# Samples' x transposed once and dt kept in three chunks, and x asked for block by block behind the first split

## The chip, the cores and the metric

The kernel runs on one core of a Trainium2 chip. The metric is the device time in microseconds (us), the median of three runs. The engines are called TensorE (PE in the profile; PEld is its weight load), VectorE (DVE), ScalarE (ACT), GpSimd (POOL) and SyncE (SP, which only issues transfers here). Each takes its instructions in order.

## The reference

One inference step of one layer with two kinds of heads, on 256 prompt tokens and 8 samples of 8 new tokens (64 rows), 320 tokens in all, width 2048, all float32:

```
h    = rms_norm(x)
proj = h @ w_in                      # columns: [gMLP u | gMLP v | SSD z | SSD x,B,C | SSD dt]
gate = gelu(u) * (tril(w_s) @ layer_norm(gelu(v)) + b_s)          # inside chunks of 128 tokens
x,B,C = silu(causal_conv4(xBC));  dt = softplus(dt_raw + dt_bias);  a = -exp(a_log)
# SSD, per head (32 heads of 64, 4 groups of 8 heads, state 128):
#   state_t = exp(dt_t a) state_{t-1} + dt_t x_t B_t^T,   y_t = state_t C_t
y    = rms_norm_by_group((y + d x) * silu(z))
x    = x + rms_norm([gate | y] @ w_out)
x    = x + rms_norm(conv_ffn(rms_norm(x)))                        # conv of 3, gelu(g)*u, d_ff 5632
```

The prompt starts from a zero state. Each sample carries its own state and runs 8 tokens; the new states (8 samples x 32 heads x 64 x 128) are outputs too.

## The kernel before

**Layout and products.** Most tiles hold features on the 128 partitions and the 320 tokens along the row (256 of the prompt, then 64 of the samples). For accuracy each big product is three: a weight block is split into `whi` (rounded) and `wlo` (the rest), the activations into `h_hi` and `h_lo`, and `accumulate` (L153 to L155) issues whi x hi, whi x lo and wlo x hi. Weights come in slabs of 512 KB through `slab` (L118 transfer on SP's queue, L124 cast on ScalarE, L125 subtraction on VectorE), with three buffers. TensorE works through the stages: v columns of `w_in` by tokens (`by_tokens`, L144), B, C, x, gate u, `w_out`, z, then the FFN. Beside the products runs a list of generators, `bg`; `tick` advances the first by one step after a part of a slab, so that small work lies between products. A scheduler then sets the order on each engine by priorities; `tc.issue_after` keeps one instruction behind another on its engine.

**The start.** `xf` is the input x, 16 blocks (`kt`) of 128 features. `load_x(k, n)` (L570) asks for n blocks from block k on ScalarE's queue. Before anything else, blocks 0, 1, 2-3 and 4-5 are asked for, four transfers; the next ones go out two blocks at a time as `x_ready` splits block `kt` into `h_hi` (ScalarE, L584) and `h_lo` (VectorE, L585), and copies the samples' columns of both into `xs_two` (L591). Ten products of ones (`early`, L70) run ahead of the first real product.

**dt.** `steps` makes dt, its decays and sums. Its products `dt_ps` (L479) bring dt to tokens in five chunks of 128: prompt, prompt, samples twice over, and, for each half of the samples (four samples of 8, 32 tokens), these 32 tokens repeated four times over the 128 partitions (`dtf`, L473). All later steps on `dt`, `dec` and `sp_e` run on 5 x 32 columns. Near its end, `dec_ps` (L539 to L546) makes the sums up to the end of a chunk, for the samples with the masks `later_s` (L544, GpSimd), one of 64x128 for each half. Just ahead of these GpSimd has the copies into `cb_cms` (L773, L774), which take over the buffer of `dacsT` and so wait for the transfer out of it.

**The SSD of a group.** `ssd(g)` (four groups) brings x to tokens. `x_of_samples(i)`, called twice per group, takes half i of the samples: ScalarE writes them fourfold into `x4` (`fourfold`, L397), TensorE transposes four blocks into `xt_ps` (L393), VectorE multiplies by dt into `xq` (L824), ScalarE rounds `xq` into `xsp[:, i]` (L841), VectorE subtracts for the lower 64 partitions (L842), so that the four quarters hold x rounded, rounded, rest, rest; two more products with dt go into `xdt`. `grown` multiplies `xsp` with the matching B parts (`bm`) into `up_ps` (L904), which is added to the samples' states `st` (L906); `with_c` forms `yo_ps` (L887). The second half's `x_of_samples(1)` stands in the first turn of the loop over the states, two steps after `x_of_samples(0)`.

Of the kernel before, what the change touches and what calls it, by code (L numbers as in the profile page):

```python
# [9 lines left out]
F32 = mybir.dt.float32  # L10
# [3 lines left out]
ALU = mybir.AluOpType  # L14
# [20 lines left out]
def hybrid_step(  # L35
# [21 lines left out]
    def misc(name):  # L57
        return ms.tile([P, 512], F32, tag="ms", name=name)
# [332 lines left out]
    def by_token(ps, x, c):  # L391

        pe.transpose(ps, x[:, P * c:P * c + P], ident)  # L393
# [6 lines left out]
    with ExitStack() as mctx:  # L400
# [40 lines left out]

        dt = op.tile([P, 5, NH], F32, name="dt")
        sums = op.tile([P, 3, NH], F32, name="sums")
        dec = op.tile([P, 5, NH], F32, name="dec")
        ed = op.tile([P, 4, 4], F32, name="ed")
        tote = op.tile([P, NH, NB], F32, name="tote")

# [17 lines left out]
        def steps():  # L467

            dtf = op.tile([P, NT + NS + 2 * P], F32, tag="dtf", name="dtf", bufs=1)
            dve.tensor_tensor(out=dtf[:, :NT], in0=ps_dt[0][:, :NT], in1=r1, op=ALU.mult)  # L470
            pool.tensor_copy(dtf[:, NT:NT + NS], dtf[:, NP:NT])
            for i in range(2):
                pool.tensor_copy(dtf[:, (3 + i) * P:(4 + i) * P].rearrange("p (q t) -> p q t", q=4),  # L473
                                 dtf[:, NP + 32 * i:NP + 32 * i + 32].unsqueeze(1).to_broadcast([P, 4, 32]))
            yield
            ps = misc("dt_ps")
            for c in range(5):

                pe.matmul(ps[:, NH * c:NH * c + NH], dtf[:, P * c:P * c + P], sums[:, 0], start=True, stop=True)  # L479
            H5 = 5 * NH  # L480
            dve.tensor_tensor(out=dt, in0=ps[:, :H5].rearrange("p (c h) -> p c h", c=5),
                              in1=bias_bc.unsqueeze(1).to_broadcast([P, 5, NH]), op=ALU.add)

            e = op.tile([P, 5, NH], F32, name="sp_e")
            q = dec
            z2 = tp.tile([P, NT], F32, tag="pv", name="sp_z2", bufs=4)[:, :5 * NH].rearrange("p (c h) -> p c h", c=5)
            act.activation(e, dt, AF.Abs)
            act.activation(e, e, AF.Exp, scale=-1.0)
            dve.tensor_scalar(out=q, in0=e, scalar1=2.0, scalar2=None, op0=ALU.add)
            dve.reciprocal(q, q)  # L490
            dve.tensor_tensor(out=e, in0=e, in1=q, op=ALU.mult)
            dve.tensor_tensor(out=z2, in0=e, in1=e, op=ALU.mult)
            dve.tensor_scalar(out=q, in0=z2, scalar1=2.0 / 17, scalar2=2.0 / 15, op0=ALU.mult, op1=ALU.add)
            for n in (13, 11, 9, 7, 5, 3, 1):
                dve.tensor_tensor(out=q, in0=q, in1=z2, op=ALU.mult)
                dve.tensor_scalar(out=q, in0=q, scalar1=2.0 / n, scalar2=None, op0=ALU.add)
            yield
            dve.tensor_tensor(out=q, in0=q, in1=e, op=ALU.mult)
            dve.scalar_tensor_tensor(out=dt, in0=dt, scalar=0.0, in1=q, op0=ALU.max, op1=ALU.add)
            da = e  # L500
            ea = a_bc
            act.activation(ea, a_bc, AF.Exp)
            dve.scalar_tensor_tensor(out=da, in0=dt, scalar=-1.0, in1=ea.unsqueeze(1).to_broadcast([P, 5, NH]),
                                     op0=ALU.mult, op1=ALU.mult)
# [12 lines left out]
            p4 = ps[:, 2 * NH:3 * NH].rearrange("p (g r i) -> p g r i", g=4, r=2)  # L517
            for r in range(2):
                x_at, s_at = slice(64 - 64 * r, P - 64 * r), slice(64 * r, 64 * r + 64)
                dve.tensor_copy(n4[x_at, :, r], p4[x_at, :, r])  # L520
                act.activation(ed[s_at], p4[s_at, :, r], AF.Exp)
            yield

            ps = misc("csT_ps")
            for c in range(2):
                pe.matmul(ps[:NH, P * c:P * c + P], da[:, c], upper, start=True, stop=True)
            pe.matmul(ps[:NH, NP:NT], da[:NS, 2], upper_s[:NS], start=True, stop=True)
            dacsT = op.tile([P, NT + NS + 2 * P], F32, tag="dtf", name="dacsT", bufs=1)[:, :NT + NS]
            dve.tensor_copy(dacsT[:NH, NS:], ps[:NH, :NT])
            dve.tensor_copy(dacsT[:NH, :NS], ps[:NH, NP:NT])  # L530
            sp.dma_start(dacs_d, dacsT[:NH])
            totc = op.tile([NH, NB], F32, name="totc")
            dve.tensor_copy(totc, dacsT[:NH, :NS].rearrange("p (b t) -> p b t", b=NB)[:, :, TS - 1])
            sp.dma_start(tot_d, totc)
            yield

            ps = misc("dec_ps")
            for c in range(2):
                pe.matmul(ps[:, NH * c:NH * c + NH], later, da[:, c], start=True, stop=True)  # L539
            pe.matmul(ps[:, 2 * NH:3 * NH], ones, da[:, 1], start=True, stop=True)  # L540
            later_s = tp.tile([P, NT], F32, tag="pv", name="later_s", bufs=4)[:NS, :2 * P].rearrange("p (r q t) -> p r q t", r=2, q=4)
            for r in range(2):
                rs = slice(32 * r, 32 * r + 32)
                pool.tensor_tensor(out=later_s[:, r], in0=later[:NS, rs].unsqueeze(1).to_broadcast([NS, 4, 32]),  # L544
                                   in1=bd[:, rs].unsqueeze(1).to_broadcast([NS, 4, 32]), op=ALU.mult)
                pe.matmul(ps[:, (3 + r) * NH:(4 + r) * NH], later_s[:, r].rearrange("p q t -> p (q t)"), da[:NS, 2],  # L546
                          start=True, stop=True)
            act.activation(dec.rearrange("p c h -> p (c h)"), ps[:, :H5], AF.Exp)
            dve.tensor_tensor(out=dt[:, 3:5], in0=dt[:, 3:5], in1=dec[:, 3:5], op=ALU.mult)

            sp.dma_start(tote, tot_d.unsqueeze(0).broadcast_to([P, NH, NB]))
            act.activation(tote, tote, AF.Exp)


        with tc.tile_pool(name="gp", bufs=1) as gp:
# [13 lines left out]
                cs = slice(KD + NT * k if k else 0, KD + NT * (k + n))  # L569
                act.dma_start(flat[:, cs], xT[:, cs])  # L570
            with tc.high_priority(offset=300000):
                for k, n in ((0, 1), (1, 1), (2, 2), (4, 2)):
                    load_x(k, n)
                    if k == 1:
                        act.activation(held, ones[:, 0:1], AF.Square)

            x_split = []

            def x_ready(k0, nk):

                with tc.high_priority(offset=100000), tc.issue_after(rounded[0]) if rounded else nullcontext():
                    for kt in range(k0, k0 + nk):
# [1 line left out]
                        x_split.append(act.activation(hT[0][:, kt, :], x, AF.Copy, scale=pre[:, kt:kt + 1]).ins)  # L584
                        dve.scalar_tensor_tensor(out=hT[1][:, kt, :], in0=x, scalar=pre[:, kt:kt + 1],  # L585
                                                 in1=hT[0][:, kt, :].bitcast(F32), op0=ALU.mult, op1=ALU.subtract)
                        if kt % 2 == 0 and kt < 10:
                            with tc.issue_after(x_split[-1]):
                                load_x(kt + 6, 2)
                        for i in range(2):  # L590
                            dve.tensor_copy(xs_two[kt // 8][:, kt % 8, NS * i:NS * i + NS], hT[i][:, kt, NP:])  # L591

# [174 lines left out]
        with tc.tile_pool(name="sd", bufs=1) as sd:  # L767
# [31 lines left out]
            def ssd(g):  # L799
# [31 lines left out]
                                       in1=dec[:, i, h0:h0 + 8].unsqueeze(2).to_broadcast([P, 8, 64]), op=ALU.mult)  # L831
                    return xde

                def x_of_samples(i):
                    ps = misc("xt_ps")
                    x4 = fourfold(sd.tile([P, 4, P], F32, tag="xde", name="x4", bufs=2), xs, i)
                    for j in range(4):
                        by_token(ps[:, P * j:P * j + P], x4[:, j], 0)
                    xq = sd.tile([P, 512], F32, tag="xde", name="xq", bufs=2)
                    times(xq, ps, 3 + i)  # L840
                    act.copy(xsp[:, i], xq)  # L841
                    dve.tensor_tensor(out=xsp[64:, i], in0=xq[64:], in1=xsp[64:, i].bitcast(F32), op=ALU.subtract)  # L842
                    for r in range(2):
                        at = slice(64 - 64 * r + 32 * i, 96 - 64 * r + 32 * i)
                        times(xdt[at, 2, 256 * r:256 * r + 256], ps[at, 256 * r:256 * r + 256], 2, at, slice(4 * r, 4 * r + 4))

                for c in range(2):
                    ps = misc("xt_ps")
# [19 lines left out]
                for hb in range(2):  # L868
                    dve.tensor_tensor(out=cms[:, 4 * hb:4 * hb + 4], in0=cmask[:, 4 * hb:4 * hb + 4],
                                      in1=cT[:, g, NP + 32 * hb:NP + 32 * hb + 32].unsqueeze(1).to_broadcast([P, 4, 32]),  # L870
                                      op=ALU.mult)
                x_of_samples(0)
                yield

                ps = misc("s1_ps")
# [56 lines left out]
                for i in range(4):  # L932
# [4 lines left out]
                    if i:  # L937
                        end(i - 1)
                    yield
                    if i == 0:  # L940
                        x_of_samples(1)
                    yield
                begin(3)
                yo_to_xdt()
# [470 lines left out]
```

## Time and profile before

| What | Value |
|---|---|
| median of three runs | 1779.02 us (1778.82 to 1779.88) |
| the profiled execution's own time | 1781.37 us |
| its span | 1779.7 us |
| TensorE, VectorE, ScalarE, GpSimd busy | 99%, 66%, 46%, 15% |
| mean DMA rate over the span | 163 GB/s |

The profile is of one execution, whose own time is its span and 1.7 us around it. A line of the timeline gives start and duration in us, engine, source line, operation, and tile written from tiles read with their shapes; in square brackets stand the idle time of the engine just before and what ended it. A merged line carries "x" and a count. One float32 product with plain float32 operands shows as two records, a transpose as one. In groups, the numbers after the bar are busy us and mean ns of one.

### The profile page before, as it was taken

The page shows a single profiled execution, that of the slowest core. Times are in us where ns is not written, and L with a number is a line of the kernel's source. Part 1 is how long each engine was busy: PE and PEld are TensorE (multiplying, and loading weights), DVE is VectorE, ACT ScalarE, POOL GpSimd, SP SyncE. Part 2 cuts the span into 40 slices and gives each one's busy share as a digit, 9 for nine tenths or more (in the row PEclk, how much of TensorE's full clock was granted, in tenths as well). Part 3 has the DMA queues.
Part 4 walks back from the last instruction along what each step waited for, and adds up shares of the span by engine and source line. Part 5 has one row for each costly group of instructions (what it writes and reads, how often), then busy time and mean ns, then how long its engine had stood idle before and what let it go on. Part 6 is the DMA issues. An engine that isn't in the chain of part 4 may idle for free.

```text
span 1779.7 us, 30655 instructions
## 1 busy us (share of the span) xinstructions
PE 1770.5 (99%) x11933; PEld 1715.7 (96%) x11933; DVE 1168.0 (66%) x1999; ACT 819.5 (46%) x1195; POOL 273.5 (15%) x602
## 2 busy tenths in 40 slices
PE   9999999999999999999999999999999999999998
PEld 7789999999999998999999999999999999999998
DVE  7549764656977768677865464756656575656575
ACT  5434555334564547445545333343434343433445
POOL 1202200000331313103121011110102020101004
PEclk9999999999999999999999999999999999999999
DMA  7546645456665665554554545545545545454543
GB/s 260 163 148 177 189 128 154 153 153 188 216 190 190 181 207 168 168 171 145 180 156 146 157 149 151 155 148 152 157 144 156 150 150 155 150 150 155 147 154 107
DMA packets 214417, 289.91 MB, mean 163 GB/s; under 512 B 16384, under 2 KB 143744, under 8 KB 214080
## 3 DMA queue, kind: packets, MB, share of 16 engines
q1 hardware_dynamic: 202544, 268.74, 49.6%
q10 hardware_dynamic: 10016, 14.16, 2.2%
q0 software_dynamic: 1712, 5.05, 1.0%
q8 instruction: 94, 1.54, 0.4%
q14 instruction: 51, 0.42, 0.1%
HBM read 273.08 MB, written 14.82 MB: 162 GB/s over the span
## 4 chain that ended last, share of the span: by engine, by line
PE 97%; DVE 1%; ACT 0%; DMA 0%; issue 0%; POOL 0%; POOLq 0%; ACTq 0%; DVEq 0%
PE ps L153 19%; PE ps L155 19%; PE ps L154 19%; PE pd L153 10%; PE pd L155 10%; PE pd L154 10%; PE ps_v L144 7%; PE y_ps L983 1%; PE up_ps L904 0%; PE yo_ps L887 0%; PE sg L731 0%; PE xt_ps L393 0%; DMA cs<-dacs_d 0%; PE x1p L1278 0%; PE tsum L296 0%
## 5 line engine op out<-in xcount | busy, mean ns | idle before, releaser
L125 DVE TENSOR_TENSOR wlo<-wraw,whi 128x1024 fp32r<-128x1024 f32 (+1 forms) x476 | 582.5, 1224 | 432.4 <-ACT whi L124 430.1
L124 ACT CAST whi<-wraw 128x1024 fp32r<-128x1024 f32 (+1 forms) x475 | 494.8, 1042 | 729.9 <-PE ps L154 392.1
L153 PE MATMUL ps<-h_hi,whi 128*128 128x320 f32 x2268 | 704.0, 311 | 0.0
L154 PE MATMUL ps<-h_lo,whi 128*128 128x320 f32 x2268 | 702.7, 310 | 0.0
L155 PE MATMUL ps<-h_hi,wlo 128*128 128x320 f32 x2268 | 702.2, 310 | 0.0
L153 PEld LDWEIGHTS ps<-h_hi,whi 128*128 128x128 f32 x2268 | 426.2, 188 | 2.6 <-issue 1.6
L154 PEld LDWEIGHTS ps<-h_lo,whi 128*128 128x128 f32 x2268 | 426.3, 188 | 0.7
L155 PEld LDWEIGHTS ps<-h_hi,wlo 128*128 128x128 f32 x2268 | 426.2, 188 | 0.0
L155 PE MATMUL pd<-fhi,wlo 128*128 128x320 f32 x704 | 218.2, 310 | 0.0
L153 PE MATMUL pd<-fhi,whi 128*128 128x320 f32 x704 | 218.2, 310 | 0.0
L154 PE MATMUL pd<-flo,whi 128*128 128x320 f32 x704 | 218.2, 310 | 0.0
L153 PE MATMUL pd<-ohi,whi 128*128 128x320 f32 x448 | 139.4, 311 | 0.0
L155 PE MATMUL pd<-ohi,wlo 128*128 128x320 f32 x448 | 138.7, 310 | 0.0
L154 PE MATMUL pd<-olo,whi 128*128 128x320 f32 x448 | 138.7, 310 | 0.0
L153 PEld LDWEIGHTS pd<-fhi,whi 128*128 128x128 f32 x704 | 132.1, 188 | 0.0
L154 PEld LDWEIGHTS pd<-flo,whi 128*128 128x128 f32 x704 | 132.1, 188 | 0.0
L155 PEld LDWEIGHTS pd<-fhi,wlo 128*128 128x128 f32 x704 | 132.1, 188 | 0.0
L1180 POOL COPY ptf<-pad 128x2 f32<-128x2 f32 x88 | 21.0, 239 | 603.7 <-DVE pad L1168 603.0
L249 DVE TENSOR_TENSOR acc_ffn<-acc_ffn,pd 128x320 f32<-128x320 f32 (+1 forms) x161 | 77.5, 482 | 37.8 <-PE pd L155 36.5
L153 PEld LDWEIGHTS pd<-ohi,whi 128*128 128x128 f32 x448 | 84.1, 188 | 1.4 <-issue 1.0
L154 PEld LDWEIGHTS pd<-olo,whi 128*128 128x128 f32 x448 | 84.1, 188 | 0.3
L155 PEld LDWEIGHTS pd<-ohi,wlo 128*128 128x128 f32 x448 | 84.1, 188 | 0.1
(328 smaller groups left out, 1867.9 us busy)
## 6 DMA issues: line engine op xcount, KB each, us to landing
wraw<-in_ffn_w_up SPq DMA_DIRECT2D x176, 512.0 KB, 3.7
wraw<-in_w_in SPq DMA_DIRECT2D x140, 512.0 KB, 3.8
wraw<-in_ffn_w_down SPq DMA_DIRECT2D x88, 512.0 KB, 3.4
wraw<-in_w_out SPq DMA_DIRECT2D x64, 512.0 KB, 3.4
st<-in_state_ssm SPq DMA_DIRECT2D x32, 256.0 KB, 3.9
out_ssm_state_sample<-st ACTq DMA_DIRECT2D x30, 256.0 KB, 3.4
cs<-dacs_d SPq DMA_DIRECT2D x16, 320.0 KB, 4.7
xr<-in_xT SPq DMA_DIRECT2D x4, 640.0 KB, 4.0
```

Source lines behind the costliest of these rows:

```text
L124: rounded[:] = [act.copy(hi, raw).ins]
L125: dve.tensor_tensor(out=lo, in0=raw, in1=hi.bitcast(F32), op=ALU.subtract)
L144: made = pe.matmul(out, xi, w[g][wi], start=first and begins, stop=last and ends)
L153: pe.matmul(ps, whi, xhi, start=first, stop=False)
L154: pe.matmul(ps, whi, xlo, start=False, stop=False)
L155: return pe.matmul(ps, wlo, xhi, start=False, stop=last).ins
L249: added_last[:] = [dve.tensor_tensor(out=acc[:, nb, ts], in0=acc[:, nb, ts], in1=ps[:, ts], op=ALU.add).ins]
L983: pe.matmul(ps[64 * i:64 * i + 64, cols], w(hl), x(hl, m, cpx), tile_position=(0, 64 * i), **flags)
L1180: pool.tensor_copy(ptf[:, k, :], pad[:, 256:258])
```

## The change

Three things change. First, `dt` keeps three chunks in `steps` (two of the prompt, one of the samples), so that its steps run on 3 x 32 columns; a fourth column of `dt` and `dec`, on 64 partitions, holds the samples' decayed dt, and there is one mask `later_s` of 64x64, made ahead of the `csT_ps` products. Second, `x_of_samples` is called once per group: it transposes the 64 sample rows directly from `xs` (outputs of 64 rows), multiplies by dt once, and then fills the four quarters of both halves of `xsp` by 32-row copies: two rounded ones, a subtraction, and a copy of the rest for each half, six copies on ScalarE and two subtractions on VectorE per group. Third, only x's block 0 is asked for ahead of its split. Blocks 1 and 2-3 are asked for behind the split of block 0, blocks 4-5 and 6-7 behind that of block 1, the others as before.

In the order in which the instructions of the two built programs stand, TensorE's differs at these places only: two `dt_ps` products fewer, one `later_s` product in the insertion of the others in place of two a product apart each, one set of four sample transposes per group for two, and `up_ps` of the first samples a little earlier in groups 1 and 3. VectorE splits `h_lo` of block 0 ahead of the first `wlo`. The number of transfers of x stays at nine.

```diff
-        dt = op.tile([P, 5, NH], F32, name="dt")
+        dt = op.tile([P, 4, NH], F32, name="dt")
...
-            for i in range(2):
-                pool.tensor_copy(dtf[:, (3 + i) * P:(4 + i) * P].rearrange("p (q t) -> p q t", q=4),
-                                 dtf[:, NP + 32 * i:NP + 32 * i + 32].unsqueeze(1).to_broadcast([P, 4, 32]))
             yield
             ps = misc("dt_ps")
-            for c in range(5):
+            for c in range(3):
                 pe.matmul(ps[:, NH * c:NH * c + NH], dtf[:, P * c:P * c + P], sums[:, 0], start=True, stop=True)
...
+            later_s = tp.tile([P, NT], F32, tag="pv", name="later_s", bufs=4)[:NS, :NS]
+            pool.tensor_tensor(out=later_s, in0=later[:NS, :NS], in1=bd, op=ALU.mult)
             ps = misc("csT_ps")
...
-            for r in range(2):
-                rs = slice(32 * r, 32 * r + 32)
-                pool.tensor_tensor(out=later_s[:, r], in0=later[:NS, rs].unsqueeze(1).to_broadcast([NS, 4, 32]),
-                                   in1=bd[:, rs].unsqueeze(1).to_broadcast([NS, 4, 32]), op=ALU.mult)
-                pe.matmul(ps[:, (3 + r) * NH:(4 + r) * NH], later_s[:, r].rearrange("p q t -> p (q t)"), da[:NS, 2],
-                          start=True, stop=True)
-            act.activation(dec.rearrange("p c h -> p (c h)"), ps[:, :H5], AF.Exp)
-            dve.tensor_tensor(out=dt[:, 3:5], in0=dt[:, 3:5], in1=dec[:, 3:5], op=ALU.mult)
+            pe.matmul(ps[:NS, 3 * NH:4 * NH], later_s, da[:NS, 2], start=True, stop=True)
+            act.activation(dec[:, :3].rearrange("p c h -> p (c h)"), ps[:, :3 * NH], AF.Exp)
+            act.activation(dec[:NS, 3], ps[:NS, 3 * NH:4 * NH], AF.Exp)
+            dve.tensor_tensor(out=dt[:NS, 3], in0=dt[:NS, 2], in1=dec[:NS, 3], op=ALU.mult)
...
-                for k, n in ((0, 1), (1, 1), (2, 2), (4, 2)):
-                    load_x(k, n)
-                    if k == 1:
-                        act.activation(held, ones[:, 0:1], AF.Square)
+                load_x(0, 1)
+                act.activation(held, ones[:, 0:1], AF.Square)
...
-                        if kt % 2 == 0 and kt < 10:
-                            with tc.issue_after(x_split[-1]):
-                                load_x(kt + 6, 2)
+                        with tc.issue_after(x_split[-1]):
+                            for k, n in ((1, 1), (2, 2)) if kt == 0 else ((4, 2), (6, 2)) if kt == 1 else ((kt + 6, 2),) if kt in (2, 4, 6, 8) else ():
+                                load_x(k, n)
...
-                def x_of_samples(i):
+                def x_of_samples():
                     ps = misc("xt_ps")
-                    x4 = fourfold(sd.tile([P, 4, P], F32, tag="xde", name="x4", bufs=2), xs, i)
                     for j in range(4):
-                        by_token(ps[:, P * j:P * j + P], x4[:, j], 0)
+                        pe.transpose(ps[:NS, P * j:P * j + P], xs[:, j, NP:NT], ident)
                     xq = sd.tile([P, 512], F32, tag="xde", name="xq", bufs=2)
-                    times(xq, ps, 3 + i)
-                    act.copy(xsp[:, i], xq)
-                    dve.tensor_tensor(out=xsp[64:, i], in0=xq[64:], in1=xsp[64:, i].bitcast(F32), op=ALU.subtract)
+                    at = slice(0, NS)
+                    times(xq[at], ps[at], 3, at)
                     for r in range(2):
-                        at = slice(64 - 64 * r + 32 * i, 96 - 64 * r + 32 * i)
-                        times(xdt[at, 2, 256 * r:256 * r + 256], ps[at, 256 * r:256 * r + 256], 2, at, slice(4 * r, 4 * r + 4))
+                        times(xdt[64 - 64 * r:P - 64 * r, 2, 256 * r:256 * r + 256], ps[at, 256 * r:256 * r + 256], 2, at,
+                              slice(4 * r, 4 * r + 4))
+                    for i in range(2):
+                        here = slice(32 * i, 32 * i + 32)
+                        for q in range(2):
+                            act.copy(xsp[32 * q:32 * q + 32, i], xq[here])
+                        dve.tensor_tensor(out=xsp[64:96, i], in0=xq[here], in1=xsp[here, i].bitcast(F32), op=ALU.subtract)
+                        act.copy(xsp[96:P, i], xsp[64:96, i])
...
-                    if i == 0:
-                        x_of_samples(1)
```

More of the change, by code (lines that the diff above doesn't have):

```diff
@@ L440, in heads_in @@
             return xs
-        dt = op.tile([P, 5, NH], F32, name="dt")
+        dt = op.tile([P, 4, NH], F32, name="dt")
         sums = op.tile([P, 3, NH], F32, name="sums")
-        dec = op.tile([P, 5, NH], F32, name="dec")
+        dec = op.tile([P, 4, NH], F32, name="dec")
         ed = op.tile([P, 4, 4], F32, name="ed")
@@ L471, in steps @@
             pool.tensor_copy(dtf[:, NT:NT + NS], dtf[:, NP:NT])
-            for i in range(2):
-                pool.tensor_copy(dtf[:, (3 + i) * P:(4 + i) * P].rearrange("p (q t) -> p q t", q=4),
-                                 dtf[:, NP + 32 * i:NP + 32 * i + 32].unsqueeze(1).to_broadcast([P, 4, 32]))
             yield
             ps = misc("dt_ps")
-            for c in range(5):
+            for c in range(3):
                 pe.matmul(ps[:, NH * c:NH * c + NH], dtf[:, P * c:P * c + P], sums[:, 0], start=True, stop=True)
[L480 to L487, printed above, removed]
+            dt3 = dt[:, :3]
+            dve.tensor_tensor(out=dt3, in0=ps[:, :3 * NH].rearrange("p (c h) -> p c h", c=3),
+                              in1=bias_bc.unsqueeze(1).to_broadcast([P, 3, NH]), op=ALU.add)
+            e = op.tile([P, 3, NH], F32, name="sp_e")
+            q = dec[:, :3]
+            z2 = tp.tile([P, NT], F32, tag="pv", name="sp_z2", bufs=4)[:, :3 * NH].rearrange("p (c h) -> p c h", c=3)
+            act.activation(e, dt3, AF.Abs)
             act.activation(e, e, AF.Exp, scale=-1.0)
@@ L498, in steps @@
             dve.tensor_tensor(out=q, in0=q, in1=e, op=ALU.mult)
-            dve.scalar_tensor_tensor(out=dt, in0=dt, scalar=0.0, in1=q, op0=ALU.max, op1=ALU.add)
+            dve.scalar_tensor_tensor(out=dt3, in0=dt3, scalar=0.0, in1=q, op0=ALU.max, op1=ALU.add)
             da = e
@@ L502, in steps @@
             act.activation(ea, a_bc, AF.Exp)
-            dve.scalar_tensor_tensor(out=da, in0=dt, scalar=-1.0, in1=ea.unsqueeze(1).to_broadcast([P, 5, NH]),
+            dve.scalar_tensor_tensor(out=da, in0=dt3, scalar=-1.0, in1=ea.unsqueeze(1).to_broadcast([P, 3, NH]),
                                      op0=ALU.mult, op1=ALU.mult)
@@ L540, in steps @@
             pe.matmul(ps[:, 2 * NH:3 * NH], ones, da[:, 1], start=True, stop=True)
-            later_s = tp.tile([P, NT], F32, tag="pv", name="later_s", bufs=4)[:NS, :2 * P].rearrange("p (r q t) -> p r q t", r=2, q=4)
-            for r in range(2):
-                rs = slice(32 * r, 32 * r + 32)
-                pool.tensor_tensor(out=later_s[:, r], in0=later[:NS, rs].unsqueeze(1).to_broadcast([NS, 4, 32]),
-                                   in1=bd[:, rs].unsqueeze(1).to_broadcast([NS, 4, 32]), op=ALU.mult)
-                pe.matmul(ps[:, (3 + r) * NH:(4 + r) * NH], later_s[:, r].rearrange("p q t -> p (q t)"), da[:NS, 2],
-                          start=True, stop=True)
-            act.activation(dec.rearrange("p c h -> p (c h)"), ps[:, :H5], AF.Exp)
-            dve.tensor_tensor(out=dt[:, 3:5], in0=dt[:, 3:5], in1=dec[:, 3:5], op=ALU.mult)
+            pe.matmul(ps[:NS, 3 * NH:4 * NH], later_s, da[:NS, 2], start=True, stop=True)
+            act.activation(dec[:, :3].rearrange("p c h -> p (c h)"), ps[:, :3 * NH], AF.Exp)
+            act.activation(dec[:NS, 3], ps[:NS, 3 * NH:4 * NH], AF.Exp)
+            dve.tensor_tensor(out=dt[:NS, 3], in0=dt[:NS, 2], in1=dec[:NS, 3], op=ALU.mult)
             sp.dma_start(tote, tot_d.unsqueeze(0).broadcast_to([P, NH, NB]))
@@ L871, in ssd @@
                                       op=ALU.mult)
-                x_of_samples(0)
+                x_of_samples()
                 yield
```

## The prediction

> **What bounds the kernel now.** I read the page first, then who waits for whom, then the busy times by stretch, and last the timeline of the places that the change touches.
>
> ```profile
> span 1779.7 us, 30655 instructions
> ...
> PE 1770.5 (99%) x11933; PEld 1715.7 (96%) x11933; DVE 1168.0 (66%) x1999; ACT 819.5 (46%) x1195; POOL 273.5 (15%) x602
> ...
> PE 97%; DVE 1%; ACT 0%; DMA 0%; issue 0%; POOL 0%; POOLq 0%; ACTq 0%; DVEq 0%
> ```
>
> TensorE is busy for 99% of the span and 97% of the chain that ended last is its own. So an instruction that TensorE no longer issues is time saved in full, work on other engines counts only where TensorE waits for it, and every new wait of TensorE counts in full. In the view of TensorE's waits, no line names a weight tile; two of them name what is edited here:
>
> ```profile
> PE dec_ps L546 <- POOL later_s L544: 1.0, 2, 0.7
> PE up_ps L904 <- DVE xsp L842: 0.8, 2, 0.6
> ```
>
> The first is 1.0 us in two waits, the second 0.8 us in two. The busy times by stretch (us, then busy time and count for PE, PEld, DVE, ACT, POOL, then granted clock, DMA share, GB/s) show what stands behind the first:
>
> ```profile
> 246.80:250.20 3.40, 3.40 (x14) 3.40 (x14) 0.22 (x1) 0.38 (x2) 0.00 (x0) 0.50 0.55 154
> 250.20:254.00 3.80, 3.80 (x28) 3.80 (x27) 1.17 (x1) 1.36 (x2) 0.00 (x0) 1.00 0.00 0
> ```
>
> For 3.4 us right after the `later_s` waits the granted clock is 0.50, and half as many products fit.
>
> **Part 1: `later_s`.** GpSimd makes two 64x128 masks behind two copies into `cb_cms` that wait for the transfer of `dacsT`. TensorE alone, then GpSimd alone:
>
> ```profile
> 243.55 0.31 PE L155 MATMUL ps<-h_hi,wlo 128*128 128x320 f32 x1
> 243.70 0.53 PE L539 MATMUL dec_ps<-sp_e,later 128*128 128x32 f32 x4
> 244.06 0.39 PE L540 MATMUL dec_ps<-sp_e,ones 128*128 128x32 f32 x2
> 244.29 0.39 PE L153 MATMUL ps<-h_hi,whi 128*128 128x320 f32 x1
> 245.02 0.41 PE L546 MATMUL dec_ps<-sp_e,later_s 64*128 64x32 f32 x2 [0.34 <-POOL later_s L544]
> 245.36 0.41 PE L154 MATMUL ps<-h_lo,whi 128*128 128x320 f32 x1
> 246.46 0.41 PE L546 MATMUL dec_ps<-sp_e,later_s 64*128 64x32 f32 x2 [0.69 <-POOL later_s L544]
> 246.80 0.63 PE L155 MATMUL ps<-h_hi,wlo 128*128 128x320 f32 x1
> ...
> 250.33 0.31 PE L153 MATMUL ps<-h_hi,whi 128*128 128x320 f32 x1
> ...
> 250.92 0.31 PE L154 MATMUL ps<-h_lo,whi 128*128 128x320 f32 x1
> ```
>
> ```profile
> 243.81 0.33 POOL L773 COPY cb_cms<-ident 64x64 f32<-64x64 f32 x1 [25.68 <-PE ps L154]
> ...
> 244.52 1.89 POOL L544 TENSOR_TENSOR later_s<-later,bd 64x128 f32<-64x128 f32 x2
> ```
>
> At full clock a product follows the last by 0.147 us (250.33 to 250.92, four steps). From 243.55 to 246.80, 3.25 us, three of them start (0.44 us), so `dec_ps` costs 2.81 us. Its first insertion, of three small products, costs 0.74 - 0.15 = 0.59 us. After the change a fourth joins it, and no other insertion follows: the smaller mask is made before the `csT_ps` products, and in the order in which the changed program's instructions stand it is ahead of both copies on a GpSimd that had been idle for 25.68 us. A fourth costs 0.21 us (a fifth of the `dt_ps` row below). Saved: 2.81 - 0.80 = **2.0 us** (1.6 if the new product has an insertion of its own, 0.58 us like the one at 245.02 without its wait).
>
> From 246.80 to 250.33 thirteen products take 3.53 us in place of 1.91: the half clock costs **1.6 us** more. A stall of 0.34 and one of 0.69 us amid small products let the clock fall; the two waits for `xsp`, 0.8 us together among full products, did not. With the stalls gone I take it as gone. The Trainium skill (TensorE: Matmul & The Clock Gate, Part 1) says that the clock is halved after an idle window of about 3.4 us, and that the window runs freely. The length agrees; idle it was not, since TensorE stood still for 1.03 us of it in all. By that rule the dip hangs on where the window lies, and is a case of its own below.
>
> **Part 2: fewer products.** From the chain that ended last, in order of time:
>
> ```profile
> 212.81 1.03 PE dt_ps L479 x10
> ...
> 448.26 0.44 PE xt_ps L393 x4
> ```
>
> `dt_ps` issues three products for five: two fifths of 1.03, **0.4 us**. Each of the four head groups transposes its samples in one set of four rather than two sets. A set takes 0.44 us; four sets are **1.8 us**. The remaining sets write 64 rows and not 128. I price them as before, 0.44 us: the columns that stream through are the same 128. Were they half as dear, 0.9 us more would go.
>
> The steps on 96 columns in place of 160, and two GpSimd copies less, I price at nothing: none of these engines is waited for there. ScalarE gets six 32-row copies per group for two whole copies and two fourfold ones; at 0.6 us each that adds some 5 us, on an engine that idles for 54% of the span. If the weight casts behind these were late, TensorE would wait for weights, which it does nowhere now.
>
> **Part 3: when TensorE gets `xsp`.** It waits in groups 1 and 3, for the second half of the samples. Now both halves come from one set of transposes, and TensorE asks for both early: in group 1 right behind `yo_ps`, 24 products after the transposes. Rows of group 1 (vector, scalar, tensor), then the subtraction over all groups (least, median and most ns), and from the page the mean ns of a weight subtraction and cast:
>
> ```profile
> 513.16 0.68 DVE L824 TENSOR_TENSOR xq<-xt_ps,dt 128x512 f32<-128x512 f32 x1
> ```
> ```profile
> 513.87 0.62 ACT L841 CAST xsp<-xq 128x512 fp32r<-128x512 f32 x1 [0.82 <-DVE xq L824]
> ```
> ```profile
> 517.54 0.60 PE L393 MATMUL xt_ps<-ident,x 128*128 128x128 f32 x4
> 518.07 0.64 PE L887 MATMUL yo_ps<-st,cb_cms 128*32 128x256 f32 x8
> ```
> ```profile
> L842 DVE TENSOR_TENSOR xsp<-xq,xsp x8: 690/1004/1445, 445.8 to 704.5; 64x512 fp32r<-64x512 f32 x8
> ```
> ```profile
> L125 DVE TENSOR_TENSOR wlo<-wraw,whi 128x1024 fp32r<-128x1024 f32 (+1 forms) x476 | 582.5, 1224 | 432.4 <-ACT whi L124 430.1
> L124 ACT CAST whi<-wraw 128x1024 fp32r<-128x1024 f32 (+1 forms) x475 | 494.8, 1042 | 729.9 <-PE ps L154 392.1
> ```
>
> The second set at 517.54 is gone and `yo_ps` (0.64) takes its place, so TensorE asks at about 518.2 and 518.4. A copy's time goes by its row of 512, not by its rows: I keep 0.62 us on ScalarE and at least 0.69 on VectorE for 32 rows. ScalarE starts at 513.87; four copies and that of `s` end at 517.0. VectorE, done with `xq` at 513.84, has a weight subtraction (1.22) and two `xdt` products of half the width (0.4 each) first; it subtracts from 515.9 and ends at 517.3. The last copy ends at 517.9, in time by 0.5 us. With both subtractions at 1.445 us it would end at 519.4, and TensorE would wait 1.0 us. The Trainium skill (GPSIMD Engine Reference, Key points) says that GpSimd shares its SBUF interfaces with VectorE, in contention when VectorE has two SBUF inputs, as these subtractions have; GpSimd is busy on `st` here. The spread of the row, 690 to 1445 ns, agrees. In group 3 a weight cast (1.04) stands ahead of the last copy; by the same steps that copy ends within 0.2 us of TensorE's asking. So the old 0.8 us of waits goes, and I put 0.1 us of new ones against it, nearer to the quiet case because GpSimd's work covers only part of the two subtractions: **0.7 us** saved, between 0.8 saved and, with 1.0 us in group 1 and 0.4 in group 3, 0.6 lost.
>
> **Part 4: the start.** ScalarE's queue, then TensorE, then the landing of the second block (KB, us from issue) and those of all x transfers of the first 24 us:
>
> ```profile
> 4.23 0.33 ACTq L570 DMA_DIRECT2D vt<-in_xT  x1
> 4.61 0.56 ACT L584 ACTIVATE h_hi<-vt 128x320 fp32r<-128x320 f32 x1 [1.37 <-DMA vt<-in_xT]
> ```
> ```profile
> 9.32 0.40 PE L144 MATMUL ps_v<-whi,h_hi 128*128 128x512 f32 x1
> 9.56 0.39 PE L144 MATMUL ps_v<-whi,h_lo 128*128 128x512 f32 x1
> ```
> ```profile
> vt<-in_xT ACTq DMA_DIRECT2D x1, 160.0 KB, 4.7
> ```
> ```profile
> DMA to landing us min/median/max: 3.4/5.1/5.7
> ```
>
> The first block lands at 4.2 (the least, 3.4, after an issue at 0.8) and its split waits until 4.61 because ScalarE first issues a transfer (4.23). That issue leaves, so the split starts at 4.25. TensorE gains 0.1 us at most, since `xs_two` now stands behind `wlo` on VectorE. The second block is asked for behind that, at 4.26, and no longer right behind the first. TensorE needs its low part at 9.5 (9.56 less the gain); it comes 1.25 us after the landing (split 0.56, low part 0.55, hand-overs), so it must land by 8.2. At 3.4 us it lands at 7.7, at its own 4.7 at 9.0, at 5.7 at 10.0. No other x transfer is ahead of it, but six weight transfers are: I take 4.1, nearer to 3.4 than to 5.7, landing at 8.4: 0.2 lost, 0.1 gained, **-0.1 us**; ends +0.1 and -1.8. All later blocks are needed 3.8 us (sixteen products at 0.24) apart and come with slack. The moved issues pass nothing on SP; on ScalarE they stand ahead of two weight casts, needed only at 11.
>
> **Sum.** 2.0 + 1.6 + 0.4 + 1.8 + 0.7 - 0.1 = 6.4 us off the profiled execution's 1781.37 (span 1779.7 and 1.7 around it). That execution is 2.35 us above the median of 1779.02; I take the same 6.4 us off the median: **1772.6**.
>
> **Rivals.** *The half clock is not in the timed executions* (or stays in others): 1779.02 - 4.8 = 1774.2. For it: the profiled one is 2.35 us slower, and 1.6 of that could be this. Against: the sparse stretch is 3.2 us long, so most placings of a 3.4 us window catch much of it. 0.25.
>
> *x comes late.* At 5.7 us the start loses 1.7 us, and a stall of that size could bring 1.6 us of half clock: 1772.6 + 3.3 = 1775.9. For it: most x landings are near 5. Against: those are 320 KB each. 0.12.
>
> *The stalls stay* (`later_s` or `xsp` late in another way), and only the products go: 1779.0 - 2.2 = 1776.8. 0.07.
>
> *Slower: the chain to `xsp` runs serially.* From the samples' transposes to the last quarter: `xq` 0.69, five copies ahead of the last two 3.1, two subtractions at 1.445, two copies 1.24, and a weight cast and subtraction between, 2.27: 10.2 us. By the places of its instructions TensorE has 66, 24, 36 and 24 products (0.147 each) and two `yo_ps` (0.64 each) in between: 11.0, 4.8, 6.6 and 4.8 us. Stalls: 0 + 5.4 + 3.6 + 5.4 = 14.4 us, against 6.7 us won elsewhere (the old waits included): 1786.7. It decides from 6.7 us of stalls on. Against it: the copies need only `xq`, so they overlap the subtractions. 0.05.
>
> **Numbers.** The forecast has 0.51; its own range is 1771.3 to 1773.7. From 1771.0 to 1776.0 the range takes in the first two rivals and leaves out most of the third, the fourth, and a tail below. A measurement of this kernel can tell about 0.2%, 3.6 us: below 1775.5 is faster. Forecast, first rival and a small part of the second: 0.79 faster; the rest of the second and the third: 0.16; slower 0.05.
>
> **What would show it.** `dec_ps` in one insertion near 244 with no wait, no 0.50 clock at 247; three `dt_ps` products; sixteen sample transposes of 64 rows; `up_ps` waits under 0.4 us in all; the second x block landing near 8.4 and TensorE without a gap at 9.3. Wrong would be a wait of `up_ps` in every group, an idle TensorE with half clock in the first 20 us, or a new wait for `whi`.

## The result, and the profile after

| Kernel | median, us | executions |
|---|---|---|
| before, timed on the same chip | 1779.66 | 22 |
| changed | 1782.61 | 22 |
| changed, the profiled execution | 1783.25 (span 1781.5) | 1 |

The ratio is 1.0014 (95%: 1.0009 to 1.0020): 3.0 us slower, a small loss but one clear of its interval, where 1772.6 had been forecast. The page of the changed kernel, and its view of TensorE's waits (us in all, times, longest):

```profile
span 1781.5 us, 30593 instructions
...
PE 1770.3 (99%) x11911; PEld 1715.3 (96%) x11911; DVE 1164.1 (65%) x1987; ACT 825.2 (46%) x1204; POOL 273.5 (15%) x599
...
PE 96%; DVE 2%; ACT 1%; DMA 1%; issue 0%; ACTq 0%; DVEq 0%
```
```profile
PE up_ps L901 <- ACT xsp L842: 3.2, 3, 2.0
...
PE y_ps L978 <- PE y_ps L978: 0.5, 1, 0.5
PE yo_ps L884 <- DMA st<-in_state_ssm: 0.2, 1, 0.2
```

The 22 records less of TensorE are there (11911 for 11933), and the `later_s` waits are gone. In their place `up_ps` waits 3.2 us in three waits for the last copy into `xsp`, where it had waited 0.8. The longest is in group 2, which Part 3 of the prediction did not walk through. VectorE, ScalarE, GpSimd and TensorE there, from the timeline:

```profile
602.94 0.68 DVE L841 TENSOR_TENSOR xsp<-xq,xsp 32x512 fp32r<-32x512 f32 x1
603.66 2.15 DVE L967 TENSOR_TENSOR cs<-cs,cb_cms 128x320 f32<-128x320 f32 x3
605.73 2.08 DVE L125 TENSOR_TENSOR wlo<-wraw,whi 128x1024 fp32r<-128x1024 f32 x1
607.73 1.34 DVE L967 TENSOR_TENSOR cs<-cs,cb_cms 128x320 f32<-128x320 f32 x1
609.10 1.48 DVE L841 TENSOR_TENSOR xsp<-xq,xsp 32x512 fp32r<-32x512 f32 x1
```
```profile
610.62 0.62 ACT L842 CAST xsp<-xsp 32x512 fp32r<-32x512 f32 x1 [3.68 <-DVE xsp L841]
```
```profile
604.11 1.35 POOL L822 TENSOR_TENSOR xde<-xdt,dec 128x512 f32<-128x512 f32 x1 [2.95 <-PE s_ps L873]
605.42 3.31 POOL L895 TENSOR_TENSOR st<-st,tote 128x512 f32<-128x512 f32 x2
608.98 2.52 POOL L895 TENSOR_TENSOR st<-st,tote 128x512 f32<-128x512 f32 x2 [0.25 <-PE yo_ps L884]
```
```profile
608.81 0.51 PE L901 MATMUL up_ps<-xsp,bm 128*128 128x512 f32 x1
611.28 0.79 PE L901 MATMUL up_ps<-xsp,bm 128*128 128x512 f32 x1 [1.97 <-ACT xsp L842]
```

The second half's subtraction stands on VectorE behind four products with `cb` and a weight subtraction. Beside GpSimd's `st` the weight subtraction takes 2.08 us (mean 1.22) and the subtraction for `xsp` 1.48 in place of 0.68. ScalarE idles 3.68 us, copies, and TensorE has stood still for 1.97 us. Then, by stretch (us, busy and count for PE, PEld, DVE, ACT, POOL, granted clock, DMA share, GB/s):

```profile
604.13:607.54 3.41, 3.41 (x28) 3.02 (x21) 3.41 (x4) 2.72 (x5) 3.41 (x3) 1.00 0.00 0
607.55:610.96 3.41, 1.77 (x15) 0.84 (x13) 3.35 (x4) 0.34 (x1) 3.16 (x3) 1.00 0.53 152
610.97:614.38 3.41, 3.10 (x11) 3.01 (x12) 2.15 (x3) 1.72 (x3) 0.53 (x1) 0.50 0.40 150
614.39:617.80 3.41, 3.41 (x27) 2.71 (x26) 0.00 (x0) 1.05 (x1) 0.44 (x1) 1.00 0.76 228
```

One stretch in which TensorE was busy for 1.77 of 3.41 us, and the next runs at half the clock. A second half-clock stretch lies in the small products at the end:

```profile
1768.09:1771.49 3.40, 3.40 (x13) 3.01 (x13) 2.72 (x7) 0.43 (x1) 1.53 (x2) 0.50 0.13 48
```

Group 1 went the way of the prediction's upper bound: both subtractions at 1.5 us, all of it beside `st`, and waits of 0.30 and 0.96 us, 1.26 in all (bound: 1.0).

```profile
512.95 3.03 DVE L841 TENSOR_TENSOR xsp<-xq,xsp 32x512 fp32r<-32x512 f32 x2
```
```profile
512.91 5.01 POOL L895 TENSOR_TENSOR st<-st,tote 128x512 f32<-128x512 f32 x4
```
```profile
515.22 0.50 PE L901 MATMUL up_ps<-xsp,bm 128*128 128x512 f32 x1 [0.30 <-ACT xsp L842]
516.68 0.50 PE L901 MATMUL up_ps<-xsp,bm 128*128 128x512 f32 x1 [0.96 <-ACT xsp L842]
```

### The profile page after: what moved, and what is told of

Its sections match the earlier page's. It is cut to its first block, busy times and chain, and to the rows that moved or that the text cites. A ratio compares the mean times of both kernels' runs of the same rounds, so it can differ in the third digit from the quotient of the medians.

```text
span 1781.5 us, 30593 instructions
## 1 busy us (share of the span) xinstructions
PE 1770.3 (99%) x11911; PEld 1715.3 (96%) x11911; DVE 1164.1 (65%) x1987; ACT 825.2 (46%) x1204; POOL 273.5 (15%) x599
## 4 chain that ended last, share of the span: by engine, by line
PE 96%; DVE 2%; ACT 1%; DMA 1%; issue 0%; ACTq 0%; DVEq 0%
PE ps L153 18%; PE ps L154 18%; PE ps L155 18%; PE pd L153 10%; PE pd L154 10%; PE pd L155 10%; PE ps_v L144 6%; PE y_ps L978 1%; DMA vt<-in_xT 0%; PE up_ps L901 0%; DVE cs L967 0%; PE sg L723 0%; PE yo_ps L884 0%; DVE wlo L125 0%; DVE xsp L841 0%
```

## The experiments

Theory A: the chain that fills `xsp` ends too late, and its waits, with the half clock behind them, eat the gain. Theory B: the late second block of x does. Each kernel ran in one of three series, with the kernel before beside it; "before" is the kernel before in that series. The changed kernel ran in a series of its own (above), so a difference from it is put as the difference between two losses or gains against before.

**The change taken apart.** Start undone (1781.24 against 1779.82 for before), start alone (1781.01), only the masks moved (1779.61), and the fill left out (1777.03).

> The changed kernel with the start of the kernel before (blocks 0, 1, 2-3 and 4-5 of x asked for ahead of the first split). Theory A (the chain that fills xsp makes TensorE wait in groups 1 and 2, 3.2 us of waits and a half clock behind the longest): only the start's 0.4 to 0.8 us come back; about 0.5 us faster than the changed kernel, still above the kernel before or level with it; the up_ps waits stay near 3 us. Theory B (the late second block of x, with half clock behind it, is the loss): the loss of 3 us goes, and the time is below the kernel before by what the removed products save, 2 us or more.

> The kernel before with the new start alone. Theory A: 0.4 to 0.9 us slower than the kernel before, the second block landing 4.7 us after its issue and TensorE waiting 0.4 us for its low part. Theory B: 3 us slower or more.

The edit of the first, and its reverse in the second, with the issues behind the splits to match:

```diff
-                load_x(0, 1)
-                act.activation(held, ones[:, 0:1], AF.Square)
+                for k, n in ((0, 1), (1, 1), (2, 2), (4, 2)):
+                    load_x(k, n)
+                    if k == 1:
+                        act.activation(held, ones[:, 0:1], AF.Square)
```

Start undone: 1.0008 of before (1.0000 to 1.0017), so 1.4 us of the 3.0 are still there. Its trace shows waits of `up_ps` of 4.8 us and two half-clock stretches, but of an execution of 1783.51 us, 2.3 above its median. Start alone: 1.0006 (0.9997 to 1.0015), 1.2 us slower by the medians. So B is not the whole loss, nor is A by this pair alone: the medians put about half on each, with intervals of some 1.5 us either way.

> The kernel before with nothing but its two masks made ahead of the csT_ps products; both products then join the first dec_ps insertion. If the prediction's first part holds: 2.81 us of insertion and waits become 1.1, 1.7 us saved in every execution, and 1.6 more in those executions whose half clock lay there: 1.7 to 3.3 us faster in the median, no wait of dec_ps. If the half clock hangs on a window that runs freely and only the profiled execution had it there: 1.7 us. If these waits were hidden after all: no change.

```diff
...
+            for r in range(2):
+                rs = slice(32 * r, 32 * r + 32)
+                pool.tensor_tensor(out=later_s[:, r], ...)
             ps = misc("csT_ps")
...
-                pool.tensor_tensor(out=later_s[:, r], ...)
```

No wait of `dec_ps` any more, and 0.2 us by the medians: 0.9998 (0.9989 to 1.0007). The 1.7 to 3.3 us that the waits seemed to cost did not show; why, the second profile of the kernel before (below) tells.

> The changed kernel with xsp filled by two 64-row copies per half straight from xq: the two subtractions and the copies of the rest are left out, so the products with x's rest are not computed. Theory A: the up_ps waits fall from 3.2 us to under 0.5, and with them 3 us of time, 4 where a half clock came behind them: 1778 to 1779.5 for a changed kernel at 1782.6, level with the kernel before or below it. Theory B: less than 0.5 us faster than the changed kernel. If instead the added ScalarE work delays the weight casts: the waits for xsp go, but the time stays within 1 us.

```diff
-                        for q in range(2):
-                            act.copy(xsp[32 * q:32 * q + 32, i], xq[here])
-                        dve.tensor_tensor(out=xsp[64:96, i], in0=xq[here], in1=xsp[here, i].bitcast(F32), op=ALU.subtract)
-                        act.copy(xsp[96:P, i], xsp[64:96, i])
+                        for q in range(2):
+                            act.copy(xsp[64 * q:64 * q + 64, i], xq[at])
```

This kernel leaves out x's rest and puts all 64 rows into each half, so its new states are not the right ones; TensorE issues as many products as in the changed kernel (11911 records). It takes 0.9981 of before (0.9972 to 0.9989), 2.8 us less where the changed kernel took 3.0 more, and no wait of `up_ps` is left. That is theory A, and more than the 3.2 us of waits: half clocks go with them (a mean granted clock of 1.000, to three digits, in 7 of 11 executions, for 3 of 22 of the changed kernel). Work on ScalarE and VectorE went too, so the kernels below, with the whole fill, have to confirm it.

**Can the chain be made to end in time?** Urgency for its last four instructions (1780.93, before 1780.26), one engine less in it (1788.22), an earlier start (1780.28), and that with the old start (1780.16).

> The changed kernel with the four instructions of each group that end the chain (two subtractions, two copies of the rest) given the urgency that the state updates have, so that weight subtractions and the products with cb no longer stand ahead of them. If order is what makes TensorE wait (in group 2 the subtraction stood behind two products with cb and a weight subtraction): the 1.97 us wait of group 2 and the half clock behind it go, 2 to 4 us faster than the changed kernel, 1778.5 to 1780.5, up_ps waits under 1.3. If the length of the chain itself, subtractions stretched by GpSimd's work, is what counts: waits near 3 us and the time within 0.7 us of the changed kernel.

```diff
+                        with first():
                             dve.tensor_tensor(out=xsp[64:96, i], ...)
                             act.copy(xsp[96:P, i], xsp[64:96, i])
```

1.0007 of before (0.9997 to 1.0016): the loss is 0.7 us where it was 3.0, so the time moved as the first alternative said. The wait that it was to remove did not go: group 1 kept one wait of 0.28 us, group 2 got a longer one. Its VectorE and TensorE:

```profile
605.60 1.21 DVE L125 TENSOR_TENSOR wlo<-wraw,whi 128x1024 fp32r<-128x1024 f32 x1
606.74 1.34 DVE L968 TENSOR_TENSOR cs<-cs,cb_cms 128x320 f32<-128x320 f32 x1
608.11 1.43 DVE L842 TENSOR_TENSOR xsp<-xq,xsp 32x512 fp32r<-32x512 f32 x1
```
```profile
PE up_ps L902 <- ACT xsp L843: 3.8, 3, 3.3
```

The order on VectorE is that of the changed kernel. A likely reason, not tested: the first copies, which the second subtraction needs, got no urgency, so the scheduler still placed it behind the same work. Of what makes up the smaller loss the trace shows the shorter waits in group 1 (0.28 us for 1.26), and that the late `yo_ps` and the last half clock of the changed kernel's profile are absent.

> The changed kernel with the last copy of each half left to VectorE as a second subtraction: one engine hand-over and 12 copies on ScalarE less, 8 subtractions on VectorE more. If the hand-over and ScalarE's queue are what counts: 1 to 2 us of up_ps waits less and as much time. If VectorE is what counts (0.7 us for a subtraction in quiet, up to 1.5 beside GpSimd): waits as before or longer, no gain or up to 2 us slower.

```diff
-                        dve.tensor_tensor(out=xsp[64:96, i], in0=xq[here], in1=xsp[here, i].bitcast(F32), op=ALU.subtract)
-                        act.copy(xsp[96:P, i], xsp[64:96, i])
+                        for q in range(2):
+                            dve.tensor_tensor(out=xsp[64 + 32 * q:96 + 32 * q, i], in0=xq[here], in1=xsp[here, i].bitcast(F32), op=ALU.subtract)
```
```profile
PE up_ps L901 <- DVE xsp L842: 7.2, 5, 2.5
PE ps L153 <- DVE acc_mix L249: 1.8, 1, 1.8
```
```profile
515.47 5.97 DVE L842 TENSOR_TENSOR xsp<-xq,xsp 32x512 fp32r<-32x512 f32 x4
```

8.0 us slower than before (1.0041, 1.0028 to 1.0053), four times the worst that was put: four subtractions of 1.5 us in a row, while a product waits for VectorE's sum. VectorE beside GpSimd is the scarce part, not the hand-over to ScalarE.

> The changed kernel with the samples' transposes ahead of the prompt's in each group, one step earlier; nothing else. Theory A: the fill has some 2 us more before TensorE asks, the up_ps waits fall under 0.5 us and the time goes to about 1777, as where the fill was left out, with the output complete. If the fill is late because its engines are late as a whole: waits of 2 us or more stay.

> The samples' transposes first, and the start of the kernel before. Theory A with 0.4 to 0.8 us for the start: about 1776.5, 3 us below the kernel before. If the start costs nothing: equal to the samples-first kernel with the new start, within 0.3 us.

```diff
+                x_of_samples()
                 for c in range(2):
                     ps = misc("xt_ps")
...
-                x_of_samples()
                 yield
```
```profile
PE s_ps L873 <- POOL xde L822: 3.4, 4, 1.2
```

No `up_ps` wait is left, as expected, but the time is that of before (1.0002, 0.9993 to 1.0011) and not 1777: now `s_ps` waits, once in each group, for the prompt's decayed x on GpSimd, which the samples had been put ahead of. Neither theory had named that. With the old start it is 0.1 us less.

**The chain between the prompt's two sets**, so that `s_ps` keeps its place, with the new start (1777.46, before 1779.86) and the old one (1776.40).

> The changed kernel with the samples' transposes between the prompt's two sets in each group, so that the product that GpSimd's first decay needs keeps its place ahead. Theory A (TensorE waits for whichever chain is started last, the fill or the decayed x of s_ps): neither s_ps nor up_ps waits over 1 us in all, 3 us less than the changed kernel and the samples-first kernel: about 1777.5. If one of the chains is too long wherever it starts: 2 us of waits or more stay and the time is at 1779.5 or above.

> The kernel with the samples' transposes between, and the start of the kernel before. If the start costs 0.4 us: about 1777.1, 0.4 below the same kernel with the new start, and 2.5 to 3 us faster than the kernel before.

```diff
                     if c == 0:
                         x0d = decayed(0, 0)
+                        x_of_samples()
...
-                x_of_samples()
                 yield
```

TensorE's waits for `xsp` in the first and the second:

```profile
PE up_ps L901 <- ACT xsp L842: 0.2, 1, 0.2
```
```profile
PE up_ps L903 <- ACT xsp L844: 0.9, 1, 0.9
```

0.9986 (0.9977 to 0.9994) and 0.9980 (0.9971 to 0.9989): the second, with the changed dt and samples, the samples' transposes between and the old start, is the fastest of all, 3.5 us below before where the changed kernel is 3.0 above. Both have the whole fill, and the first differs from the changed kernel by nothing but the place of the samples' transposes: with the waits gone, so is the loss. The old start is worth 1.1 us here by the medians, 0.1 in the pair above, 1.2 alone: its size is not settled beyond that.

**The kernel before once more, and its masks made slower.**

> The kernel before, unchanged: a second profile of it. If its waits for later_s and the half clock behind them belong to each execution: two waits of 0.34 and 0.69 us again and a half clock for 3.4 us next to them. If the half clock hangs on where a free window lies: the waits again, and the half clock elsewhere or nowhere, the full clock's first opening at another place than 4.45 us. If the waits differ between executions: waits that are shorter or gone.

> The kernel before with each of its two GpSimd mask products made twice over, so that the later_s products come about 0.95 and 1.9 us later. If TensorE stands still for them in each execution: 1.9 us slower, and more half clocks behind it, up to 3.5 slower. If in most executions these waits are hidden, as the lack of a gain from the early masks suggests: less than 1 us slower.

In its second profile (1779.47 us) the waits for `later_s` are not there, nor a half clock before the last product. GpSimd and TensorE:

```profile
244.23 0.86 POOL L544 TENSOR_TENSOR later_s<-later,bd 64x128 f32<-64x128 f32 x2
```
```profile
243.67 0.31 PE L155 MATMUL ps<-h_hi,wlo 128*128 128x320 f32 x1
...
244.41 0.39 PE L153 MATMUL ps<-h_hi,whi 128*128 128x320 f32 x1
244.74 0.40 PE L546 MATMUL dec_ps<-sp_e,later_s 64*128 64x32 f32 x2
245.07 0.41 PE L154 MATMUL ps<-h_lo,whi 128*128 128x320 f32 x1
245.41 0.41 PE L546 MATMUL dec_ps<-sp_e,later_s 64*128 64x32 f32 x2
...
246.15 0.31 PE L154 MATMUL ps<-h_lo,whi 128*128 128x320 f32 x1
```

What differs is the landing of `dacsT`, on which the copies ahead of the masks wait; in the first profile and in this one:

```profile
DMA to landing us min/median/max: 2.9/2.9/2.9
```
```profile
DMA to landing us min/median/max: 2.4/2.4/2.4
```

At 2.4 us the masks start at 244.23 and both are made by 245.1, as VectorE turns to its next weight subtraction (245.0); at 2.9 us they started at 244.52, the second ran beside that subtraction, and the two took 1.89 us for 0.86. The trace of the kernel with the start alone, whose masks stand as before, repeats the first profile: a landing after 2.9 us, the same two waits, a half-clock stretch (1.6 us after the second wait has ended, 0.3 in the first profile), in an execution of 1783.03 us, 2.0 above its median.

```profile
PE dec_ps L546 <- POOL later_s L544: 1.0, 2, 0.7
```

With the masks made twice over,

```diff
+                pool.tensor_tensor(out=later_s[:, r], ...)   # the same product again
```
```profile
PE dec_ps L548 <- POOL later_s L546: 1.5, 1, 1.5
```
```profile
243.59:247.00 3.41, 1.90 (x15) 1.53 (x13) 2.06 (x4) 3.15 (x5) 3.13 (x6) 1.00 0.65 192
247.01:250.42 3.41, 3.41 (x13) 3.35 (x14) 0.23 (x1) 0.30 (x1) 0.00 (x0) 0.50 0.57 154
```

it is 2.9 us slower (1.0018, 1.0009 to 1.0026): 1.5 of wait and 1.6 of half clock make 3.1. So a wait there is paid in full where it occurs. The mean granted clock of each execution bounds how often a half-clock stretch does: in three digits it is below 1.000 in all 11 of this kernel, and of before in 7 of 33 in the first series, 8 of 27 in the second, and 7 of 33 and 3 of 11 in the third: 25 of 104. That is at most one in four, since a half clock behind the last product counts as well: the second profile of before has 0.999 from one. In the first series the 26 executions of before at 1.000 have a median of 1779.58, the nine of the kernel with the early masks 1779.57. All three traces with the waits have the half clock behind them, so the waits are taken to be as rare as it is; no trace shows them without it. Of the changed kernel's 22, 3 have 1.000 (median 1780.14), 11 have 0.999 (1782.33) and 8 have 0.998 (1783.62).

## Why the prediction was wrong

**Part 1** read the right mechanism from an execution that, by the clocks above, was not the usual one. In the second profile, without the waits, `dec_ps` costs 1.74 us (243.67 to 246.15, 2.48, less five steps of 0.147) and not 2.81; in the changed kernel's one insertion it costs 1.0 (244.07 to 245.52 below, 1.45, less three steps). Saved: 0.7 for 2.0. With the masks moved alone it costs 1.3 by the trace, 0.4 saved, which agrees with the 0.2 measured. The fourth product costs 0.22 us (244.90 to 245.12), as put:

```profile
244.07 0.31 PE L155 MATMUL ps<-h_hi,wlo 128*128 128x320 f32 x1
...
244.90 0.30 PE L540 MATMUL dec_ps<-sp_e,later_s 64*64 64x32 f32 x2
245.12 0.41 PE L153 MATMUL ps<-h_hi,whi 128*128 128x320 f32 x1
...
245.52 0.31 PE L155 MATMUL ps<-h_hi,wlo 128*128 128x320 f32 x1
```

**The half clock**, 1.6 us, was absent from at least three in four executions of before. The first rival said so and had 0.25; it kept the waits, which the second profile lacks too. The step that failed is "the same 6.4 us off the median": the profiled execution's 2.35 us above the median was that stall and its half clock, and should have come off first. With the terms of Part 1 this is 2.9 of the 6.4 us forecast (1.3 and 1.6).

**Part 2** held. Between the second profile of before and the changed kernel, by the same products' starts, TensorE gains 0.45 us at `dt_ps` (put: 0.4) and 0.3 to 0.5 a group, 1.65 in all, waits left aside, at the samples' transposes (put: 0.44 and 1.8). A set of 64 rows is not dearer or cheaper than one of 128: in group 0 an insertion of either costs 0.5 us.

**Part 3** is the term that turned the sign: put at 0.7 saved with an end at 0.6 lost, it lost 2.4 us in waits (3.2 for 0.8), and 1.1 in the half clock of group 2, with 0.5 more where the second `up_ps` product stands by itself at that clock. Two steps of it failed. It took 0.69 us for a subtraction, "nearer to the quiet case", where GpSimd's `st` covered the whole of both in group 1. And it walked through groups 1 and 3 only; in group 2 VectorE's order put 5.6 us of other work between the two subtractions. The fourth rival, a chain that runs serially, came nearest, at 3.2 us of stalls and not 14.4, in two of the four groups; but the copies did overlap, as was held against it, and what ran late was VectorE's part. (The 6.7 us that it sets against the stalls are 6.5 by the prediction's own terms: 5.8 less 0.1, and 0.8.) The Trainium skill (SBUF — State Buffer, SBUF: two separate sides) says that a VectorE instruction with two SBUF inputs and a GpSimd one that reads SBUF exclude each other for the whole instruction. The trace agrees with the sign: 0.68 us with GpSimd idle, 1.48 beside `st`; it would have spoken for the upper price.

**Part 4**: the second block landed 4.74 us after its issue at 4.40, not 4.1, and TensorE waited for its low part. The chain that ended last, and TensorE:

```profile
4.40 4.74 DMA vt<-in_xT
...
9.76 0.56 DVE h_lo L577
```
```profile
9.86 0.43 PE L144 MATMUL ps_v<-whi,h_hi 128*128 128x512 f32 x1
10.37 0.50 PE L144 MATMUL ps_v<-whi,h_lo 128*128 128x512 f32 x1
```

0.5 us lost at the second block, inside the bounds, five times the value taken; no half clock followed. In the seven profiles of kernels with this start the block took 4.1 to 4.7 us, so 4.1 was the least and not the middle. The second rival's 1.7 did not come. The 0.1 us put as gained at the first block did not show: its products ran 0.4 us behind those of the second profile of before.

**Not foreseen**: in group 3 a `yo_ps` is held up by a state's transfer, 1.39 us to the next large product for the usual 0.6, 0.8 lost; and the half clock in the last small products costs 0.9.

```profile
715.17 0.62 PE L884 MATMUL yo_ps<-st,cb_cms 128*32 128x256 f32 x2
716.00 0.63 PE L884 MATMUL yo_ps<-st,cb_cms 128*32 128x256 f32 x6 [0.21 <-DMA st<-in_state_ssm]
716.56 0.41 PE L153 MATMUL ps<-h_hi,whi 128*128 128x320 f32 x1
```

**The sum again**, from the second profile of before (1779.47): 0.7 + 0.45 + 1.65 saved; 2.4 of waits, 1.1 + 0.5 of half clock in group 2, 0.5 at the second block, 0.8 and 0.9 lost, 6.2 in all: 3.4 us slower. The profiled execution is 3.8 slower; the rest is the 0.4 us of the first block, where the two profiles of before start 0.3 apart themselves. For the kernel with the transposes between and the old start the same steps give 0.7 + 0.45 + 1.65 and the old waits less the new, 0.8 - 0.9: 2.7 us saved, measured 3.5 (2.0 to 5.2).

## What to carry to other kernels

Before a stall of one profile is counted as gain, ask what its length hangs on: one that comes from a transfer's landing can be absent from most executions, and a profiled time above the median says that something in it is. When several engines hand a tile on, follow the chain through each of its occurrences, at the prices that its neighbours on the other engines impose, because the longest is where the order of the queue differs. And when a chain is moved forward, look at what it is moved past.

## What the runs showed of the hardware

A half-clock stretch among the products always lasted 3.413 us or twice that, and the two of one trace are whole multiples apart ((1768.08 - 610.97) / 3.4133 = 339.0). It needed no idle stretch: TensorE was busy for 1.77 and 1.90 us of the 3.41 before it. The Trainium skill (TensorE: Matmul & The Clock Gate, Part 1) has such a window of 3413 ns that runs freely, which agrees; that it must be idle, as the page's table puts it, does not. So a stall cost its own length, or up to 1.6 us more where one half-clock stretch followed: 1.21 us in the samples-first kernel brought none, 1.5 us with the masks made twice brought one in the profile and, as a mean clock below 1.000 in each suggests, in the other executions.

A transfer that took 0.5 us longer to land (2.9 for 2.4) had the masks start 0.3 us later; that became 1.03 us of stall, since the late GpSimd work then met VectorE's, and 1.6 us of half clock behind that. This is what two profiles of one kernel differ by; that the landing is the cause is read from the order of the two traces, and no run changed the landing alone.
